# Encoder layer on one core: merged one-hot instructions, a bfloat16 position compare, 48 instead of 60 spilled u tiles, and two more raw buffers

## The chip, the core and the metric

The kernel runs on one core of a Trainium2 chip, and the metric is device time of one execution in microseconds (us). The core has five engines, each with its own instruction queue that runs strictly in order: PE (TensorE, matrix products; PEld is its loading of weights), DVE (VectorE), ACT (ScalarE), POOL (GpSimd) and SP (SyncE, which here only issues DMAs). Semaphores make an instruction wait for another engine or for a DMA. Of several runs the median counts.

## The reference, cut to what matters

One layer for 512 tokens and 16 meta tokens, model width 1024: a projection, two groups of attention-like heads, an output projection, and then PEER, a product-key lookup over 128 x 128 experts, which takes most of the time:

```
q = (x @ w_q).reshape(n, 8, 2, 128)
s = einsum('nhpc,hpkc->nhpk', q, sub_keys)
ts, ti = top_k(s, 16)                                  # per head, two halves
cand = ts[:,:,0,:,None] + ts[:,:,1,None,:]             # 16 x 16 sums
best_s, best_p = top_k(cand, 16)
idx  = (row index) * 128 + (column index)              # 16 experts per head
gate = softmax(best_s)
act  = gelu(einsum('nd,nhkd->nhk', x, u[idx]))
y    = einsum('nhk,nhkd->nd', gate * act, v[idx])
```

## The kernel before, in words

The first 128 tokens ("sparse quarter") are done as written: for each of 128 expert slots a row of u (later of v) per token is gathered by an indirect DMA that POOL issues (line 251, tile `gat`), and DVE multiplies and sums it (line 265 for u, line 263 for v). The other 384 tokens ("dense") are done for all 16,384 experts. u and v are cut into 128 tiles of 128 experts. A u tile gives 24 matmuls (lines 127 to 129) and a gelu on ACT (line 1055); a v tile gives 18 (lines 1080 to 1084). What weighs the experts is W, a dense matrix with the gates of the chosen experts and zeros elsewhere.

Precision: each fp32 operand is split in a high part (`hi`, cast on ACT, line 114) and a rest (`lo`, line 116), so each product is three matmuls. For the u tiles below `LA` the `lo` subtraction runs on POOL, for the others on DVE. A raw u tile comes by a DMA on SP's queue (line 108, `raw`, two buffers, given back when `lo` is done).

W is built 8 tokens at a time, 48 steps ("W steps", in `wbuild`). DVE compares row and column index of each choice with 0..127 (line 993, `oh<-iT,ioh`, two instructions of 128x1024 in fp16: one-hots), multiplies the first one-hot by the low and the high part of the gate (lines 994 and 996; in every fourth step the high part is done by ACT, line 999). PE multiplies the one-hots (lines 1021, 1022), ACT evacuates (line 1024, into `stg`), and after four steps a DMA on SP's queue stores `stg` to W_d in HBM (line 1026). The one-hots have four buffers.

Where the indices come from: `topk2` is called four times. In each, the position of a choice is compared with 0..15 (line 231, `eq`, 128x2048, fp32 inputs, twice per call) to pick the index.

Order of the second half of the program: the query products with their top-16 searches, then the *u phase* (u tiles 0 to LA-1 with their results spilled to A_d in HBM, and the W steps spread between them), then *v alone* (v tiles 0 to LA-1, which load W and A back), and then *u and v* (each v tile from LA on together with its u tile, nothing spilled). Before, LA is 60. No v tile can run before W is complete, six u tiles (`ET`) are kept for the end of that wait. The sparse quarter's 256 gathers are metered: RA per u tile in the u phase, RV per v tile while i < LA, RUV afterwards.

The row 0..127 that the one-hots are compared with is `iof` (64 KB, loaded on SP's queue, line 949). It lives in a pool, `wk`, whose memory is that of the query stage's score tiles, so its load waits until the last top-16 search has read them.

The order within an engine's queue is made by a scheduler at build time, from the order in which the program is written; the engines then keep it.

Of the kernel before, what the change touches and what calls it, by code (L numbers as in the profile page):

```python
# [9 lines left out]
F32 = mybir.dt.float32  # L10
# [14 lines left out]
P = 128  # L25
# [9 lines left out]
PH = 8  # L35
# [13 lines left out]
WL = 1  # L49
SC = 16  # L50
TK = 1, 1, 1, 1
# [10 lines left out]
VG = 6  # L62
RA = 0.4
RV = 0.85
RUV = 2.85
LA = 60
NCAND = 80
# [15 lines left out]
def _emit(ctx, tc, I, out):  # L83
# [105 lines left out]
    def topk2(a, b, sm, cand, tf, eq, zs):  # L189
# [35 lines left out]
        nc.vector.tensor_add(cf, cf, t1)  # L225
        nc.vector.tensor_sub(cf, cf, t9)
        nc.vector.tensor_scalar(rf, rf, -1.0, 0.0, op0=ALU.add, op1=ALU.max)
        nc.vector.tensor_add(rf, rf, t9)
        yield
        for j, pos in enumerate((rf, cf)):  # L230
            nc.vector.tensor_tensor(eq, pos[:, :, :, None].to_broadcast([P, PH, TOPK, TOPK]),
                                    io16[:, None, None, :].to_broadcast([P, PH, TOPK, TOPK]), op=ALU.is_equal)
            nc.vector.tensor_mul(eq, eq, tf[:, :, j, None, :].to_broadcast([P, PH, TOPK, TOPK]))
            nc.vector.tensor_add(eq[:, :, :, :8], eq[:, :, :, :8], eq[:, :, :, 8:])
            nc.vector.tensor_add(eq[:, :, :, :4], eq[:, :, :, :4], eq[:, :, :, 4:8])
            nc.vector.tensor_add(eq[:, :, :, :2], eq[:, :, :, :2], eq[:, :, :, 2:4])
# [710 lines left out]
    ioh = wk.tile([P, NK, QI], F16, name="ioh")  # L947
    iof = wk.tile([P, NK], F32, name="iof")
    nc.sync.dma_start(out=iof, in_=I["iota"].to_broadcast([P, NK]))
    nc.vector.tensor_copy(ioh, iof[:, :, None].to_broadcast([P, NK, QI]))  # L950
# [10 lines left out]
    def wbuild():  # L961
# [8 lines left out]
        def prep(t, m0):  # L970
            if m0 == 0:
                tr = bank((P, 3, P), tag="p")
                for j in range(3):
                    nc.tensor.transpose(out=tr[:, j, :], in_=sel[:, j, t].rearrange("p h r -> p (h r)"), identity=ident)
                gT = wk2.tile([P, P], F32, name="gT")
                nc.scalar.activation(gT, tr[:, 0, :], AF.Copy, scale=GS)
                iT = wk2.tile([P, 2, P], F16, name="iT")
                nc.scalar.copy(iT, tr[:, 1:3, :])
                gh = wk2.tile([P, P], F16, name="gh")
                nc.vector.tensor_copy(gh, gT)  # L980
                gl = wk2.tile([P, P], F16, name="gl")
                nc.vector.tensor_sub(gl, gT, gh)
                cur[t] = gT, iT, gh, gl
            gT, iT, gh, gl = cur[t]
            sh = [P, OB // QI, NK, QI]

            def tok(v):
                return v[:, m0:m0 + OB].rearrange("p (g q) -> p g q", q=QI)[:, :, None, :].to_broadcast(sh)

            oh = big.tile([P, 4] + sh[1:], F16, name="oh", tag=("hi0", "hi1", "lo0", "lo1")[(t * P + m0) // OB % WB])  # L990
            o12, ol, od = oh[:, :2], oh[:, 2], oh[:, 3]
            for j in range(2):
                nc.vector.tensor_tensor(o12[:, j], tok(iT[:, j]), ioh[:, None, :, :].to_broadcast(sh), op=ALU.is_equal)  # L993
            nc.vector.tensor_mul(ol, o12[:, 0], tok(gl))  # L994
            if m0 // OB % DM < DN:
                nc.vector.tensor_mul(od, o12[:, 0], tok(gh))  # L996
            else:
# [7 lines left out]
        for n, (t, m0) in enumerate(steps):  # L1005
# [19 lines left out]
            if q0 + OB == BL:  # L1025
                nc.sync.dma_start(out=W_d[:, ((t - 1) * P + m0) // BL], in_=stg)
            yield 2.2

    U, V = {}, {}
    gelus = []  # L1030

    def u_split(i):
        if i < NK and i not in U:
            U[i] = stream(I["uT"][i], eng=nc.gpsimd if i < LA and i % PU != PU - 1 else None)

# [232 lines left out]
```

## Time and profile before

| | us |
|---|---|
| runs: median (lowest to highest of 3) | 1678.32 (1671.53 to 1680.73) |
| the profiled execution: its own time | 1682.47 |
| the profiled execution: span from first to last instruction | 1680.7 |
| PE busy / DVE busy / ACT busy / POOL busy, of the span | 1574.4 / 1291.4 / 739.6 / 677.1 |

A profiled execution gives each instruction's start and end, what ended the idle time in front of it, and the granted TensorE clock (mean 0.973 of full speed here). A busy PE is not a PE at its peak, since matmuls overlap; the pace of PE is read from how many matmuls fall in a stretch. An instruction that is held up by another engine after it has started counts as busy: its duration is longer than that of its equals.

### The profile page before, as it was taken

Reading aid. Unit: us, or ns where it says so; the run is one execution under the profiler, and the core shown is the slowest. Engines: PE = TensorE matmul, PEld = TensorE weight load, DVE = VectorE, ACT = ScalarE, POOL = GpSimd, SP = SyncE. Lnnn points to the kernel's source line nnn. Section 1 sums busy time; section 2 is a strip of 40 time slices with the busy share of each in tenths; the row PEclk is TensorE's granted clock in tenths of the full one; section 3 lists DMA queues with packets and bytes.
Section 4 is the critical chain, followed back from the end, with each engine's and each line's share of the span. In section 5 each row is a group of like instructions: output and inputs, shape, how many; then the busy total and the mean of one; then the engine's idle time right before and its main releaser. Section 6 shows DMA issues by size and latency. Waiting matters only on the chain.

```text
span 1680.7 us, 24243 instructions
## 1 busy us (share of the span) xinstructions
PE 1574.4 (94%) x8793; PEld 1392.4 (83%) x8793; DVE 1291.4 (77%) x2529; ACT 739.6 (44%) x1229; POOL 677.1 (40%) x465
## 2 busy tenths in 40 slices
PE   6999998989986789979989999999999999999998
PEld 6888886768876689878978888889999999988996
DVE  3888768647999998948247777778887888778777
ACT  5454555543324474867533333333333333333334
POOL 3443112076334467475411212154545444344442
PEclk9999999989997989999999999999999999999999
DMA  6112222232224557656999999899999998999885
GB/s 232 54 46 81 69 61 69 84 118 89 78 73 149 176 193 250 239 218 252 328 366 342 326 314 326 278 313 389 321 329 326 336 327 315 319 339 327 308 276 185
DMA packets 152360, 387.42 MB, mean 231 GB/s; under 512 B 12752, under 2 KB 71376, under 8 KB 150576
## 3 DMA queue, kind: packets, MB, share of 16 engines
q1 hardware_dynamic: 106160, 238.79, 41.2%
q0 software_dynamic: 36864, 134.23, 22.8%
q10 hardware_dynamic: 9216, 12.85, 2.1%
q8 instruction: 69, 1.13, 0.3%
q14 instruction: 51, 0.42, 0.1%
HBM read 342.56 MB, written 40.63 MB: 228 GB/s over the span
## 4 chain that ended last, share of the span: by engine, by line
PE 28%; issue 18%; DVE 12%; POOL 10%; DMA 6%; ACT 3%; SPq 1%; POOLq 0%; ACTq 0%; DVEq 0%
POOL gat L251 7%; PE banka L1080 4%; PE banka L1083 4%; PE banka L1084 4%; POOL lo L116 3%; PE bankp L1080 2%; PE bankp L1083 2%; PE bankp L1084 2%; PE bankg L129 2%; DMA gat<-v,idx 2%; PE bankg L127 2%; PE bankg L128 2%; DMA raw<-uT 2%; DVE oh L993 2%; DMA gat<-u,idx 1%
## 5 line engine op out<-in xcount | busy, mean ns | idle before, releaser
L116 POOL TENSOR_TENSOR lo<-raw,hi 128x1024 fp32r<-128x1024 f32 x81 | 238.4, 2947 | 228.8 <-ACT hi L114 220.4
L114 ACT CAST hi<-raw 128x1024 fp32r<-128x1024 f32 x177 | 185.8, 1051 | 289.6 <-PE bankg L128 159.1
L127 PE MATMUL bankg<-un_hi,hi 128*128 128x384 f32 x880 | 300.1, 341 | 12.2 <-ACT act L1055 12.2
L129 PE MATMUL bankg<-un_hi,lo 128*128 128x384 f32 x880 | 299.6, 341 | 5.3 <-POOL lo L116 5.2
L128 PE MATMUL bankg<-un_lo,hi 128*128 128x384 f32 x880 | 297.9, 338 | 0.0
L251 POOL DMA_INDIRECT gat<-u,idx x128 | 157.8, 1232 | 299.5 <-PE bankp L1084 252.1
L251 POOL DMA_INDIRECT gat<-v,idx x128 | 167.8, 1311 | 207.6 <-PE bankp L1084 180.4
L263 DVE SCALAR_TENSOR_TENSOR acc<-gat,sact,acc 128x1024 f32<-128x1024 f32 x128 | 164.2, 1283 | 72.2 <-DMA gat<-v,idx 61.6
L265 DVE CUSTOM_DVE_ANT_0 gat<-gat,hn 128x1024 f32<-128x1024 f32 x128 | 162.9, 1282 | 53.2 <-DMA gat<-u,idx 53.1
L127 PEld LDWEIGHTS bankg<-un_hi,hi 128*128 128x128 f32 x880 | 168.1, 191 | 16.1 <-ACT act L1055 12.5
L135 DVE TENSOR_TENSOR vhl<-vraw,vhl 128x1024 fp32r<-128x1024 f32 x128 | 157.1, 1228 | 30.9 <-ACT vhl L134 30.8
L129 PEld LDWEIGHTS bankg<-un_hi,lo 128*128 128x128 f32 x880 | 167.9, 191 | 8.1 <-POOL lo L116 6.8
L128 PEld LDWEIGHTS bankg<-un_lo,hi 128*128 128x128 f32 x880 | 167.7, 191 | 3.4
L134 ACT CAST vhl<-vraw 128x1024 fp32r<-128x1024 f32 x128 | 134.2, 1049 | 46.3 <-PE bankp L1084 33.4
L116 DVE TENSOR_TENSOR lo<-raw,hi 128x1024 fp32r<-128x1024 f32 x96 | 117.8, 1228 | 24.2 <-ACT hi L114 23.0
L1024 ACT ACTIVATE stg<-banka 128x512 f32<-128x512 f32 x96 | 96.2, 1140 | 1.7 <-PE banka L1022 0.9
L993 DVE TENSOR_TENSOR oh<-iT,ioh 128x1024 f16<-128x1024 f16 x96 | 80.8, 888 | 2.4 <-PE banka L1022 2.4
L1021 PE MATMUL banka<-oh 128*128 128x128 f16 x384 | 55.3, 233 | 22.1 <-DVE oh L996 12.7
L1055 ACT ACTIVATE act<-bankg 128x384 f32<-128x384 f32 x110 | 53.4, 486 | 23.2 <-PE bankg L129 12.1
L1021 PEld LDWEIGHTS <-oh 128*128 128x128 f16 x384 | 39.2, 104 | 20.8 <-DVE oh L996 15.0
L1022 PE MATMUL banka<-oh 128*128 128x128 f16 x384 | 54.3, 233 | 0.7 <-DVE oh L994 0.7
L129 PE MATMUL bankp<-un_hi,lo 128*128 128x384 f32 x144 | 48.7, 338 | 4.5 <-POOL lo L116 4.5
(2283 smaller groups left out, 3906.3 us busy)
## 6 DMA issues: line engine op xcount, KB each, us to landing
raw<-uT SPq DMA_DIRECT2D x128, 512.0 KB
vraw<-v SPq DMA_DIRECT2D x128, 512.0 KB
W_d<-stg SPq DMA_DIRECT2D x12, 2048.0 KB
wa<-W_d SPq DMA_DIRECT2D x32, 768.0 KB
A_d<-act ACTq DMA_DIRECT2D x60, 192.0 KB
wa<-A_d SPq DMA_DIRECT2D x15, 768.0 KB
raw<-wq SPq DMA_DIRECT2D x16, 512.0 KB
raw<-win_n SPq DMA_DIRECT2D x12, 512.0 KB
```

The lines of the kernel that those rows point to most:

```text
L114: nc.scalar.copy(hi, raw)
L116: (eng or nc.vector).tensor_sub(lo, raw, hi.bitcast(F32))
L127: nc.tensor.matmul(o, lhsT=ah, rhs=bh, start=start, stop=False)
L128: nc.tensor.matmul(o, lhsT=ah, rhs=bl, start=False, stop=False)
L129: return nc.tensor.matmul(o, lhsT=al, rhs=bh, start=False, stop=stop)
L134: last[0] = nc.scalar.copy(hi, src).ins.name
L135: (eng or nc.vector).tensor_sub(lo, src, hi.bitcast(F32))
L251: g = nc.gpsimd.indirect_dma_start(out=r, out_offset=None, in_=src, in_offset=bass.IndirectOffsetOnAxis(ap=idx[:, hk:hk + 1], axis=0))
L263: nc.vector.scalar_tensor_tensor(acc0, r, sact[:, hk:hk + 1], acc0, op0=ALU.mult, op1=ALU.add)
L265: nc.vector.tensor_tensor_reduce(r, r, hn0, scale=1.0, scalar=0.0, op0=ALU.mult, op1=ALU.add, accum_out=sact[:, hk:hk + 1])
L993: nc.vector.tensor_tensor(o12[:, j], tok(iT[:, j]), ioh[:, None, :, :].to_broadcast(sh), op=ALU.is_equal)
L1080: m0 = nc.tensor.matmul(o, lhsT=gh_[:, tc_], rhs=vh[:, dc], start=(j == 0), stop=False, skip_group_check=True)
```

## The change

Seven edits:

1. `topk2`: the positions and the row 0..15 (`io16b`) are bfloat16, so both inputs and the output of the `eq` compare are 16 bit.
2. W steps: the two compares become one instruction of 128x2048; the two multiplies become one of 128x2048, except in every fourth step, where ACT still does the high part and DVE the low one (128x1024). The gates' two parts lie in one tile, `gs`.
3. LA 60 to 48. The metering of gathers goes from RA 0.4, RUV 2.85 to RA 0.15, RUV 2.7.
4. W_d stores are issued on ACT's queue.
5. `iof` moves to the pool `w1`, which lasts to the end of the program, and is loaded just ahead of the keys; the score tiles `sc` go from 16 to 15 buffers.
6. Odd u tiles from 9 to 41 are loaded into `rawx`, two more buffers in the pool `wk`.
7. A raw u tile is asked for four tiles ahead in the u phase (two before).

```diff
-SC = 16
+SC = 15
-RA = 0.4
+RA = 0.15
-RUV = 2.85
-LA = 60
+RUV = 2.7
+LA = 48
...
-        nc.vector.tensor_sub(cf, cf, t9)
+        nc.vector.tensor_sub(cb, cf, t9)
...
-        nc.vector.tensor_add(rf, rf, t9)
+        nc.vector.tensor_add(rb, rf, t9)
-        for j, pos in enumerate((rf, cf)):
+        for j, pos in enumerate((rb, cb)):
             nc.vector.tensor_tensor(eq, pos[:, :, :, None].to_broadcast([P, PH, TOPK, TOPK]),
-                                    io16[:, None, None, :].to_broadcast([P, PH, TOPK, TOPK]), op=ALU.is_equal)
+                                    io16b[:, None, None, :].to_broadcast([P, PH, TOPK, TOPK]), op=ALU.is_equal)
...
+    nc.vector.tensor_copy(io16b, io16)
...
+    iof = w1.tile([P, NK], F32, name="iof")
+    nc.sync.dma_start(out=iof, in_=I["iota"].to_broadcast([P, NK]))
     keys = qs.tile([P, 2 * PH, NK], F32, name="keys")
...
-    iof = wk.tile([P, NK], F32, name="iof")
-    nc.sync.dma_start(out=iof, in_=I["iota"].to_broadcast([P, NK]))
...
-            for j in range(2):
-                nc.vector.tensor_tensor(o12[:, j], tok(iT[:, j]), ioh[:, None, :, :].to_broadcast(sh), op=ALU.is_equal)
-            nc.vector.tensor_mul(ol, o12[:, 0], tok(gl))
-            if m0 // OB % DM < DN:
-                nc.vector.tensor_mul(od, o12[:, 0], tok(gh))
+            nc.vector.tensor_tensor(o12, tok(iT[:, blk].rearrange("p j m -> p (j m)")),
+                                    ioh[:, None, :, :].to_broadcast([P, 2 * GQ, NK, QI]), op=ALU.is_equal)
...
+            if blk % DM < DN:
+                nc.vector.tensor_mul(oh[:, 2 * GQ:].rearrange("p (c g) k q -> p c (g k q)", c=2).rearrange("p c (g k q) -> p c g k q", k=NK, q=QI),
+                                     o12[:, None, 0].to_broadcast([P, 2] + sh[1:]),
+                                     gs[:, blk].rearrange("p c (g q) -> p c g q", q=QI)[:, :, :, None, :].to_broadcast([P, 2] + sh[1:]))
             else:
+                nc.vector.tensor_mul(ol, o12[:, 0], tok(gs[:, blk, 1]))
...
-                nc.sync.dma_start(out=W_d[:, ((t - 1) * P + m0) // BL], in_=stg)
+                nc.scalar.dma_start(out=W_d[:, ((t - 1) * P + m0) // BL], in_=stg)
...
+    def u_fetch(i):
+        if i < NK and i not in U and i not in R:
+            if i % 2 and 8 <= i < LA - ET:
+                R[i] = wk.tile([P, 1024], F32, name="rawx", bufs=2)
+                nc.sync.dma_start(out=R[i], in_=I["uT"][i])
+            else:
+                R[i] = fetch(I["uT"][i])
...
         u_split(i + 2)
+        if i + 4 < LA:
+            u_fetch(i + 3)
+            u_fetch(i + 4)
```

The scheduler's order of the queues shows the edits at two places.

SP's queue before, where the u phase begins: loads of raw u tiles, and among them the load of the index row `iof`, which waits for DVE and PE (the names in brackets are the semaphores waited for).

```order
L108 DMA raw<-uT 128x1024 [waits DMAHW3_49,Pool_49]
L108 DMA raw<-uT 128x1024 [waits DMAHW4_49,Pool_49]
L949 DMA iof<-iota 128x128 [waits DVE_49,PE_49]
L108 DMA raw<-uT 128x1024 [waits DMAHW6_49,Pool_49]
L108 DMA raw<-uT 128x1024 [waits DMAHW5_49,DMAHW0_49,Pool_49]
```

The same place now, again after seven raw u tiles:

```order
L108 DMA raw<-uT 128x1024 [waits DMAHW4_49,Pool_49]
L108 DMA raw<-uT 128x1024 [waits DMAHW5_49,Pool_49]
L1047 DMA rawx<-uT 128x1024 [waits DVE_49,PE_49]
L1047 DMA rawx<-uT 128x1024
L108 DMA raw<-uT 128x1024 [waits DMAHW7_49,Pool_49]
L108 DMA raw<-uT 128x1024 [waits DMAHW1_49,Pool_49]
```

`iof` is gone from here, and in its row stands the first load into `rawx`, with a wait for the same two engines, since `rawx` lies in the same pool.

DVE's queue before, at the second of the three token tiles of W (`gh`, `gl` are the gates' parts, `oh` the one-hots, `gat` the gathered rows):

```order
L265 ISA gat,sact<-gat,hn_70 128x1024
L265 ISA sact 128x1
L980 CAST gh<-gT 128x128
L993 TENSOR_TENSOR oh<-iT,ioh 128x1024
L982 TENSOR_TENSOR gl<-gT,gh 128x128
L993 TENSOR_TENSOR oh<-iT,ioh 128x1024 x7
L996 TENSOR_TENSOR oh<-oh,gh 128x1024
L994 TENSOR_TENSOR oh<-oh,gl 128x1024
L265 ISA gat,sact<-gat,hn_70 128x1024
L265 ISA sact 128x1
```

The same place now:

```order
L985 CAST gs<-gT 128x16x8
L999 TENSOR_TENSOR oh<-iT,ioh 128x2048
L986 TENSOR_TENSOR gs<-gT,gs 128x16x8
L999 TENSOR_TENSOR oh<-iT,ioh 128x2048 x3
L1004 TENSOR_TENSOR oh<-oh,gs 128x2048 x3
L1008 TENSOR_TENSOR oh<-oh,gs 128x1024
L999 TENSOR_TENSOR oh<-iT,ioh 128x2048
L268 ISA gat,sact<-gat,hn_70 128x1024
L268 ISA sact 128x1
L999 TENSOR_TENSOR oh<-iT,ioh 128x2048
```

Four compares stand where eight stood, and gathers are used more rarely: three between the first and the last one-hot instruction of the program, fifteen before. In PE's queue 574 matmuls of u tiles stand between the first and the last matmul of the W steps, 895 before; ahead of the first stand 410, 377 before.

## Rows read from the trace of the kernel before

**Rows 1.** The page: busy time of each engine; PE and DVE in 40 slices
```profile
PE 1574.4 (94%) x8793; PEld 1392.4 (83%) x8793; DVE 1291.4 (77%) x2529; ACT 739.6 (44%) x1229; POOL 677.1 (40%) x465
...
PE   6999998989986789979989999999999999999998
...
DVE  3888768647999998948247777778887888778777
...
PEclk9999999989997989999999999999999999999999
```

**Rows 2.** Busy time by stretch: stretch, length, busy us (instructions), clock, DMA share, GB/s
```profile
474.00:558.00 84.00, 57.70 (x300) 55.73 (x299) 81.64 (x390) 27.09 (x37) 32.63 (x14) 0.82 0.33 107
558.00:804.00 246.00, 215.54 (x1644) 206.12 (x1644) 210.09 (x242) 163.58 (x259) 150.57 (x53) 0.95 0.64 230
816.00:836.00 20.00, 20.00 (x118) 20.00 (x117) 3.28 (x2) 7.62 (x10) 8.51 (x4) 1.00 1.03 362
846.00:1110.00 264.00, 263.82 (x1174) 220.32 (x1175) 193.09 (x279) 96.67 (x134) 50.41 (x50) 0.99 0.93 320
1125.00:1440.00 315.00, 315.00 (x1595) 286.90 (x1594) 259.91 (x327) 112.35 (x154) 151.57 (x111) 1.00 0.94 335
```

**Rows 3.** DVE's groups, 558 to 804: busy us, mean ns | idle before, its end
```profile
L993 DVE TENSOR_TENSOR oh<-iT,ioh 128x1024 f16<-128x1024 f16 x96 | 80.8, 888 | 2.4 <-PE banka L1022 2.4
L994 DVE TENSOR_TENSOR oh<-oh,gl 128x1024 f16<-128x1024 f16 x48 | 43.4, 908 | 0.0
L996 DVE TENSOR_TENSOR oh<-oh,gh 128x1024 f16<-128x1024 f16 x36 | 33.2, 924 | 0.0
L265 DVE CUSTOM_DVE_ANT_0 gat<-gat,hn 128x1024 f32<-128x1024 f32 x15 | 26.2, 1745 | 30.6 <-DMA gat<-u,idx 30.6
L233 DVE TENSOR_TENSOR eq<-eq,tf 128x2048 bf16<-128x2048 bf16 x4 | 7.0, 1739 | 0.1
L234 DVE TENSOR_TENSOR eq<-eq 128x1024 bf16<-128x1024 bf16 x4 | 6.9, 1727 | 0.1
L231 DVE TENSOR_TENSOR eq<-sm_cf,io 128x2048 bf16<-128x2048 f32 x2 | 4.6, 2286 | 0.0
L231 DVE TENSOR_TENSOR eq<-sm_rf,io 128x2048 bf16<-128x2048 f32 x2 | 4.6, 2277 | 0.0
```

**Rows 4.** Single lines' durations, ns: shortest/median/longest, first and last start
```profile
L993 DVE TENSOR_TENSOR oh<-iT,ioh x96: 672/679/3277, 558.8 to 802.7; 128x1024 f16<-128x1024 f16 x96
...
L265 DVE CUSTOM_DVE_ANT_0 gat<-gat,hn x16: 1207/1226/3424, 567.2 to 809.1; 128x1024 f32<-128x1024 f32 x16
...
L116 POOL TENSOR_TENSOR lo<-raw,hi x56: 2342/2434/12507, 473.1 to 830.2; 128x1024 fp32r<-128x1024 f32 x56
...
L233 DVE TENSOR_TENSOR eq<-eq,tf x8: 1211/1270/3301, 462.4 to 642.9; 128x2048 bf16<-128x2048 bf16 x8
```

**Rows 5.** DVE in order of time, 587 to 589: start us, us, instruction
```profile
587.28 1.28 DVE L993 TENSOR_TENSOR oh<-iT,ioh 128x1024 f16<-128x1024 f16 x2
588.48 0.68 DVE L994 TENSOR_TENSOR oh<-oh,gl 128x1024 f16<-128x1024 f16 x1
```

**Rows 6.** POOL's groups, 558 to 804
```profile
L116 POOL TENSOR_TENSOR lo<-raw,hi 128x1024 fp32r<-128x1024 f32 x38 | 133.3, 3513 | 85.8 <-ACT hi L114 77.5 <-PE banka L1022 8.2
```

**Rows 7.** SP's queue, 474 to 804: who waited for whom: us, times, longest
```profile
SPq L1026 <- ACT stg L1024: 24.6, 9, 8.2
SPq L949 <- DVE tiv L187: 21.3, 1, 21.3
```

**Rows 8.** The engines' waits, 558 to 804
```profile
ACT hi L114 <- DMA raw<-uT: 32.4, 11, 5.5
```

**Rows 9.** ACT's queue in order of time, 475: an issue of an A_d store
```profile
474.84 0.35 ACTq L1057 DMA_DIRECT2D A_d<-act  x1
```

**Rows 10.** DVE in order of time at the start, with the idle time before
```profile
21.01 0.79 DVE L330 SCALAR_TENSOR_TENSOR act_lo<-xT,ln,act_hi 128x528 fp32r<-128x528 f32 x1 [7.40 <-ACT act_hi L329]
```

**Rows 11.** Busy time by stretch: PE during two W steps
```profile
600.42:602.24 1.82, 1.82 (x33) 1.81 (x33) 1.82 (x2) 1.80 (x3) 1.82 (x2) 1.00 0.08 7
```

**Rows 12.** The chain of waits within 558 to 804, by line
```profile
by line: POOL lo L116 17.8%; issue 17.1%; DMA raw<-uT 12.0%; DVE oh L993 11.2%; DMA gat<-u,idx 6.3%; ACT stg L1024 3.6%; PE bankg L129 3.2%; PE bankg L127 3.0%; ACT oh L999 2.9%; PE banka L1021 2.8%; PE bankg L128 2.8%; ACT hi L114 2.8%; PE
```

More of the change, by code (lines that the diff above doesn't have):

```diff
@@ L155, in _emit @@
     io16 = cst.tile([P, TOPK], F32, name="io16")
+    io16b = cst.tile([P, TOPK], BF, name="io16b")
     def half(name, tag, j, n):
@@ L218, in topk2 @@
         cf = sm("cf")
+        rb = sm("rb", BF)
+        cb = sm("cb", BF)
         nc.vector.tensor_copy(rf, row)
@@ L976, in prep @@
                 nc.scalar.activation(gT, tr[:, 0, :], AF.Copy, scale=GS)
[L977 to L985, printed above, removed]
@@ L987, in tok @@
-            def tok(v):
-                return v[:, m0:m0 + OB].rearrange("p (g q) -> p g q", q=QI)[:, :, None, :].to_broadcast(sh)
-            oh = big.tile([P, 4] + sh[1:], F16, name="oh", tag=("hi0", "hi1", "lo0", "lo1")[(t * P + m0) // OB % WB])
-            o12, ol, od = oh[:, :2], oh[:, 2], oh[:, 3]
-            for j in range(2):
-                nc.vector.tensor_tensor(o12[:, j], tok(iT[:, j]), ioh[:, None, :, :].to_broadcast(sh), op=ALU.is_equal)
-            nc.vector.tensor_mul(ol, o12[:, 0], tok(gl))
@@ L995, in prep @@
-            if m0 // OB % DM < DN:
-                nc.vector.tensor_mul(od, o12[:, 0], tok(gh))
+                iT = wk2.tile([P, P // OB, 2, OB], F16, name="iT")
+                nc.scalar.copy(iT.rearrange("p b j m -> p j b m"), tr[:, 1:3, :].rearrange("p j (b m) -> p j b m", m=OB))
+                gs = wk2.tile([P, P // OB, 2, OB], F16, name="gs")
+                g8 = gT.rearrange("p (b m) -> p b m", m=OB)
+                nc.vector.tensor_copy(gs[:, :, 0, :], g8)
+                nc.vector.tensor_sub(gs[:, :, 1, :], g8, gs[:, :, 0, :])
@@ new lines, in prep @@
+                cur[t] = gT, iT, gs
+            gT, iT, gs = cur[t]
+            GQ = OB // QI
+            sh = [P, GQ, NK, QI]
+            def tok(v):
+                n = v.shape[1] // QI
+                return v.rearrange("p (g q) -> p g q", q=QI)[:, :, None, :].to_broadcast([P, n, NK, QI])
+            oh = big.tile([P, 4 * GQ, NK, QI], F16, name="oh", tag=("hi0", "hi1", "lo0", "lo1")[(t * P + m0) // OB % WB])
+            o12 = oh[:, :2 * GQ]
+            blk = m0 // OB
+            nc.vector.tensor_tensor(o12, tok(iT[:, blk].rearrange("p j m -> p (j m)")),
+                                    ioh[:, None, :, :].to_broadcast([P, 2 * GQ, NK, QI]), op=ALU.is_equal)
@@ new lines, in prep @@
+            o12 = o12.rearrange("p (j g) k q -> p j g k q", j=2)
+            od, ol = oh[:, 2 * GQ:3 * GQ], oh[:, 3 * GQ:]
+            if blk % DM < DN:
+                nc.vector.tensor_mul(oh[:, 2 * GQ:].rearrange("p (c g) k q -> p c (g k q)", c=2).rearrange("p c (g k q) -> p c g k q", k=NK, q=QI),
+                                     o12[:, None, 0].to_broadcast([P, 2] + sh[1:]),
+                                     gs[:, blk].rearrange("p c (g q) -> p c g q", q=QI)[:, :, :, None, :].to_broadcast([P, 2] + sh[1:]))
@@ L1025, in wbuild @@
             if q0 + OB == BL:
-                nc.sync.dma_start(out=W_d[:, ((t - 1) * P + m0) // BL], in_=stg)
+                nc.scalar.dma_start(out=W_d[:, ((t - 1) * P + m0) // BL], in_=stg)
             yield 2.2
-    U, V = {}, {}
+    U, V, R = {}, {}, {}
     gelus = []
+    def u_fetch(i):
[5 more added lines that the diff above has]
+                R[i] = fetch(I["uT"][i])
     def u_split(i):
         if i < NK and i not in U:
-            U[i] = stream(I["uT"][i], eng=nc.gpsimd if i < LA and i % PU != PU - 1 else None)
+            u_fetch(i)
+            U[i] = stream(I["uT"][i], raw=R.pop(i), eng=nc.gpsimd if i < LA and i % PU != PU - 1 else None)
     def v_split(i):
```

## The prediction

> **What bounds the kernel now.** I read the page first, then the busy time by stretch, then the waits and the single lines inside the one stretch that is not bound by PE.
>
> The page has PE busy 94% of the span, and its slices show where it isn't: around the middle third, where DVE's slices are full [rows 1]. The stretches say it sharper [rows 2]. From 846 on (v alone) PE is busy 263.8 of 264 us, and from 1125 on (u and v) 315.0 of 315. There one v tile with one u tile is 42 matmuls, and 1595 matmuls in 315 us make 8.29 us a pair. The u phase alone shows 118 matmuls in 20.00 us, so 24 of them take 4.07. I take 4.15, half a pair, for a u tile, wherever it stands. So behind the u phase the time is PE's work alone, and each u tile that is moved there costs 4.15 us in full.
>
> In the W stretch, 558 to 804 (first to last one-hot instruction, 246 us), DVE is busy 210.1 us, and what it lacks is nearly all one wait: 30.6 us for gathered rows [rows 2, 3]. DVE is in order, so a gather that comes late stops the one-hots behind it, and they stop PE's W matmuls. But its busy time is not all its own. A one-hot takes 679 ns at the median and 3277 at the longest, 2.6 us more, about one `lo` on POOL (median 2434, longest 12507) [rows 4]. The two engines hold each other up. Counted over the means, DVE's stretching is (888-679)x96 + (908-679)x48 + (924-679)x36 + (1745-1226)x15 + (1739-1211)x4 + (1727-679)x4 ns = 54 us, spread over 38 `lo` of POOL, 1.42 us each [rows 3, 4, 6]. So the W stretch is DVE's own work, plus what POOL takes from it, plus the waits for gathers.
>
> **The change part by part.** The sum is made against the profiled execution, 1682.5 us, of which the span is 1680.7. It lies 4.2 us above the median of the runs, 1678.3.
>
> *The bfloat16 compare.* A compare of 128x2048 with fp32 inputs takes 2.28 us, the multiply of the same size with 16-bit operands 1.21 at the shortest [rows 3, 4]. That is 1.07 us each, four times before the W stretch and four times in it: 4 us each. DVE has 81.6 of 84 us busy before the stretch [rows 2], so both count.
>
> *One-hots.* 48 pairs of compares and 36 pairs of multiplies become 84 instructions of twice the size. By durations a pair gives back 2x0.679 - 1.21 = 0.15 us, 12 us in all. By starts it is less: two follow each other within 1.20 us though each lasts 0.68 [rows 5], and if the large one overlaps its successor by the same 0.08, it takes 1.13. That is 0.07 us a pair, 6 us. I take 6, since the pace counts and not the duration. The bounds are 0 and 12.
>
> *Fewer gathers in the W stretch.* DVE's order holds 3 there for 15. Twelve fewer at 1.23 us are 15 us of work. Their waits, 12/15 of 30.6 us, are 24 us. The gathers move to the last stage, where DVE has 260 of 315 us busy and PE is the bound [rows 2], and cost nothing there: RUV 2.7 over 80 tiles keeps less per tile than 2.85 over 68.
>
> *Thirteen u tiles fewer in the W stretch.* PE's order holds 574 u matmuls between first and last W matmul for 895, 13.4 tiles. So POOL has some 25 `lo` there for 38. At 1.42 us each that gives DVE back 18 us. But POOL did part of its work while DVE stood waiting for gathers, and with those waits gone that work falls on DVE too. I take 12 us, bounds 0 and 32 (13 times the whole 2.43).
>
> The Trainium skill's page "SBUF — State Buffer", section "SBUF: two separate sides", says that VectorE with two SBUF inputs and GpSimd share one port pair under an exclusive lock that is held for a whole instruction. The longest one-hot, its own 0.68 and a whole `lo`, agrees; by that rule in full the term is 32 and not 12, which is the first rival below.
>
> *The price: 12 u tiles behind the u phase.* 12 x 4.15 = +50 us, all on PE, which has no idle time there. Their spills to A_d and back fall away, and they lie beside PE's work in both places, 0.
>
> *Stores on ACT's queue.* SP stood 24.6 us in nine waits for the last part of `stg`, with raw loads behind it [rows 7]. ACT now issues the twelve stores behind its own evacuation, at about 0.35 us each [rows 9], 4 us beside 163.6 of 246 us busy [rows 2]; nothing on its queue waits longer than that. SP's gain is a raw load that comes earlier. ACT waited 32.4 us for raw tiles in the stretch [rows 8], and those loads are 12% of its chain [rows 12], but DVE lost no time other than to gathers and POOL, so I count 0. The cover is DVE's work: if it shrinks further than I think, PE's tiles show next.
>
> *Two more buffers, four tiles ahead.* For the same reason 0. And one wait changes its name only: SP stood 21.3 us at the load of `iof`, until the last top-16 search gave its score tile free [rows 7]. Now the first `rawx` load stands in that very place with the same wait, and all raw loads stand behind it as before. I count nothing for moving `iof`.
>
> *Small things.* The new copy `io16b` waits for its DMA in DVE's queue ahead of the last parts of the input, where DVE is idle 7.40 us [rows 10]: 0. Fifteen score buffers: the sixteenth copy waits for the first tile's readers, first in DVE's order: 0.
>
> *Sum.* Before the stretch -4. In it -6 -4 -15 -24 -12 = -61, so that 246 becomes 185. Behind it +50. Together -15: 1667.5 for such an execution, and less the 4.2, 1663 for the median.
>
> **The rivals.**
>
> *A: each `lo` takes its whole 2.43 us from DVE, or the raw loads were on the path.* POOL's 13 `lo` are worth 32 us, the stretch becomes 165, and the time 1643. For it: the longest one-hot, and POOL and raw loads as two of the three largest parts of the chain [rows 4, 12]. Against it: DVE's stretching measured 1.42 us a `lo`, not 2.43 [rows 3, 6].
>
> *B: PE becomes the floor of the W stretch.* Two W steps take PE 1.82 us [rows 11], 48 take 44. Before, 37.3 u tiles at 4.15 make 155, together 199 of 246 us, so 47 were lost to waiting in order. Now 23.9 tiles make 99, with W 143; if the same 47 are lost, and the first W matmul comes 6 us later since 410 u matmuls stand ahead of it and not 377, the stretch takes 196. That is -50 in place of -61: 1674, no change. For it: u and W matmuls share one in-order queue. Against it: most of the lost time was DVE's lateness, which is what shrinks.
>
> *C: slower. DVE waits in another place.* With longer instructions DVE keeps POOL out longer, `lo` comes late, PE's tile stands in front of the W matmuls, and the four one-hot buffers come free late. Then gathers' waits turn into waits for PE, and POOL's share gives nothing: only 6 + 4 + 15 = 25 us are left in the stretch. -4 -25 +50 = +21: 1699. It decides from the point where the stretch shrinks by less than 46 us, to over 200. Against it: DVE waited for PE only 2.4 us in 96 one-hots [rows 3]. For it: a `lo` was already held up to 12.5 us [rows 4].
>
> *D: the change does not do what it says.* The merged forms and the new compare take 2.28 us, like the fp32 compare of that size. 84 x 2.28 + 12 x 0.68 = 200 us for 122, and nothing from the compare: some +85 on 1663, 1748. Against it: the present one-hot has the same inner pair of elements and takes 0.68 us for half the size [rows 4, 5].
>
> **How the numbers follow.** My forecast (1650 to 1676) gets 0.50, A 0.18, B 0.18, C 0.10, D 0.04. The forecast is 1663. The measurement of this kernel can tell about 0.5% from no change, 8.4 us: faster is under 1670, slower over 1687. Faster: 0.8 of the forecast, A, and a little of B, 0.61. Slower: most of C, D and a little of B, 0.13. The same: 0.26. The range for 8 in 10 runs from A's middle, a little below it, to between B and C: 1638 to 1690. The terms' own bounds (0 to 12, 0 to 32) lie inside.
>
> **What the changed profile would show.** The W stretch, first to last one-hot instruction, at 185 us, under 200 in any case for a gain; merged one-hots at about 1.2 us at the median, the compare also; DVE's wait for gathers there under 8 us; still one raw load with a wait of some 20 us on DVE near 480; the stages behind at 8.29 us a pair and PE without idle time. A median of 2.2 us at the one-hots would be D; waits of DVE for PE in the tens of us C. If the stretch takes 165 or less, my term for POOL was too small. If u and v together take more than 8.4 us a pair, the price is wrong.

## The result: slower by 0.9%, and the profile after

The changed kernel takes 1691.81 us (median of 5 runs, 1691.65 to 1695.35), beside 1678.32 for the kernel before (1671.53 to 1680.73). The ratio over all runs is 1.0093, 95% interval 1.0069 to 1.0118 (the medians alone give 1.0080). I had forecast 1663, with a range up to 1690: the sign was wrong, and the time lies outside the range.

The profiled execution after takes 1691.9 us, its span is 1690.1. The page of the changed kernel, the same lines as [rows 1]:

```profile
PE 1584.6 (94%) x8793; PEld 1397.7 (83%) x8793; DVE 1281.3 (76%) x2458; ACT 737.7 (44%) x1229; POOL 637.9 (38%) x453
...
PE   7999999989976868997999999999999999999998
...
DVE  3888767647999978891577778877777787777786
...
PEclk9999997989998888999999999999999999999999
```

The middle part in which PE isn't full is shorter, and the full part behind it longer. I cut both executions at the same four events, each read from its instructions in order of time: the end of the first u tile's gelu, the first one-hot, the last one-hot, the first v matmul.

| part of the span, us | before | after | change | forecast |
|---|---|---|---|---|
| up to the first gelu | 474.8 | 479.1 | +4.3 | 0 |
| first gelu to first one-hot | 84.0 | 94.8 | +10.8 | -4 |
| first to last one-hot | 245.2 | 186.9 | -58.3 | -61 |
| last one-hot to first v matmul | 42.2 | 40.1 | -2.1 | 0 |
| first v matmul to the end | 834.5 | 889.2 | +54.7 | +50 |
| span | 1680.7 | 1690.1 | +9.4 | -15 |

The W stretch came within 3 us of the forecast, and the kernel is slower all the same. The second row shows why this proves less than it seems: the stretch begins where DVE gets to its first one-hot, and DVE gets there later. The busy time by stretch after (stretch, length, then busy us of PE, PEld, DVE, ACT and POOL, clock, DMA share, GB/s), to be read beside [rows 2]:

```profile
479.00:574.00 95.00, 66.49 (x345) 64.67 (x344) 95.00 (x392) 29.26 (x40) 40.10 (x15) 0.84 0.34 116
574.00:761.00 187.00, 161.13 (x1343) 152.48 (x1342) 161.63 (x129) 146.18 (x233) 91.75 (x28) 0.94 0.59 217
801.00:1010.00 209.00, 209.00 (x926) 174.51 (x927) 152.19 (x221) 76.29 (x105) 38.07 (x38) 0.99 0.92 320
1040.00:1440.00 400.00, 398.01 (x2004) 360.10 (x2003) 312.99 (x403) 140.40 (x195) 168.37 (x130) 1.00 0.90 319
```

DVE is busy 95.00 of 95 us ahead of the one-hots. With 392 instructions there as against 390 before, it takes 13 us more for as many. DVE's groups between the first and the last one-hot, beside [rows 3] (busy us, mean ns | idle before, its end):

```profile
L999 DVE TENSOR_TENSOR oh<-iT,ioh 128x2048 f16<-128x2048 f16 x48 | 67.9, 1442 | 0.0
L1004 DVE TENSOR_TENSOR oh<-oh,gs 128x2048 f16<-128x2048 f16 x36 | 64.5, 1818 | 0.1
L1008 DVE TENSOR_TENSOR oh<-oh,gs 128x1024 f16<-128x1024 f16 x12 | 12.6, 1047 | 0.1
L268 DVE CUSTOM_DVE_ANT_0 gat<-gat,hn 128x1024 f32<-128x1024 f32 x4 | 4.9, 1216 | 12.1 <-DMA gat<-u,idx 12.1
```

Single lines' durations after (ns: shortest/median/longest, first and last start), beside [rows 4]:

```profile
L999 DVE TENSOR_TENSOR oh<-iT,ioh x48: 1203/1211/3457, 574.0 to 758.9; 128x2048 f16<-128x2048 f16 x48
...
L1004 DVE TENSOR_TENSOR oh<-oh,gs x36: 1209/1212/3466, 580.8 to 755.5; 128x2048 f16<-128x2048 f16 x36
...
L234 DVE TENSOR_TENSOR eq<-sm_rb,io16b x4: 2268/2276/4384, 462.9 to 585.2; 128x2048 bf16<-128x2048 bf16 x4
L234 DVE TENSOR_TENSOR eq<-sm_cb,io16b x4: 2271/3280/4489, 481.8 to 621.8; 128x2048 bf16<-128x2048 bf16 x4
...
L116 POOL TENSOR_TENSOR lo<-raw,hi x52: 2349/2402/12819, 34.2 to 811.1; 128x1024 fp32r<-128x1024 f32 x52
```

The merged one-hots take 1.21 us, as forecast. The bfloat16 compare takes 2.28 where nothing holds it up, as the fp32 one did: all its operands have 16 bits now, and it gained nothing. The longest compare and one-hots still lie 2.2 us over those times, nearly a `lo` of POOL.

Two more views, the waits of DVE between the first gelu and the last one-hot, and of SP's queue there (us, times, longest), beside [rows 3, 7]:

```profile
DVE gs L985 <- ACT gT L980: 12.8, 2, 7.2
DVE gat L268 <- DMA gat<-u,idx: 12.1, 1, 12.1
```

```profile
SPq L108 <- POOL lo L116: 127.8, 20, 20.7
SPq L1047 <- POOL lo L116: 109.1, 15, 19.4
SPq L1047 <- DVE tiv L188: 21.3, 1, 21.3
```

The gathers' wait is 12.1 us, not under 8, and another has grown beside it: DVE waits 12.8 us for ACT to copy the transposed gates, 2.5 before. The first raw load into the new buffers (L1047) has inherited the 21.3 us, as forecast. And SP's other loads wait for POOL, which has not used the buffers yet: asking earlier doesn't help where the reader is late.

The +4.3 at the front is there by 304 us already (a load of `wo` that SP issues at 303.8 before and at 308.0 after), and PE's clock goes with it. Ten microseconds well before the u phase, first of the kernel before, then after:

```profile
280.00:290.00 10.00, 10.00 (x39) 6.59 (x38) 6.11 (x15) 6.36 (x20) 0.00 (x0) 0.83 0.05 11
```

```profile
280.00:290.00 10.00, 10.00 (x28) 6.53 (x28) 4.14 (x10) 4.22 (x13) 0.00 (x0) 0.50 0.00 1
```

The granted clock is 0.50 here after, the lower of its two levels (1.2 GHz), and a full-busy PE does 28 matmuls for 39. By their starts, the same matmuls stand 1.4 us earlier after than before near 270 us, and 4.3 us later from some 300 on.

### The profile page after: what moved, and what is told of

Read it like the earlier page. It is cut to its first block, busy times and chain, and to the rows that moved or that the text cites. A ratio compares the mean times of both kernels' runs of the same rounds, so it can differ in the third digit from the quotient of the medians.

```text
span 1690.1 us, 24084 instructions
## 1 busy us (share of the span) xinstructions
PE 1584.6 (94%) x8793; PEld 1397.7 (83%) x8793; DVE 1281.3 (76%) x2458; ACT 737.7 (44%) x1229; POOL 637.9 (38%) x453
## 4 chain that ended last, share of the span: by engine, by line
issue 24%; PE 15%; POOL 9%; DVE 8%; DMA 6%; ACT 2%; SPq 1%; POOLq 0%; ACTq 0%; DVEq 0%
POOL gat L254 9%; DMA gat<-v,idx 3%; DVE oh L999 3%; PE banka L1104 2%; PE banka L1100 2%; PE banka L1103 2%; DMA gat<-u,idx 2%; DVE oh L1004 2%; PE bankg L129 1%; PE bankg L128 1%; PE bankg L127 1%; PE bankp L1103 1%; PE bankp L1100 1%; PE bankp L1104 1%; DVE gat L268 1%
## 5 line engine op out<-in xcount | busy, mean ns | idle before, releaser
L127 PE MATMUL bankg<-un_hi,hi 128*128 128x384 f32 x912 | 310.2, 340 | 17.1 <-ACT act L1075 17.1
L129 PE MATMUL bankg<-un_hi,lo 128*128 128x384 f32 x912 | 310.2, 340 | 6.6 <-POOL lo L116 6.6
L128 PE MATMUL bankg<-un_lo,hi 128*128 128x384 f32 x912 | 309.4, 339 | 0.0
L114 ACT CAST hi<-raw 128x1024 fp32r<-128x1024 f32 x160 | 168.0, 1051 | 214.8 <-PE bankg L128 136.2
L116 POOL TENSOR_TENSOR lo<-raw,hi 128x1024 fp32r<-128x1024 f32 x52 | 151.3, 2911 | 174.0 <-ACT hi L114 160.2
L116 DVE TENSOR_TENSOR lo<-raw,hi 128x1024 fp32r<-128x1024 f32 x108 | 132.4, 1226 | 17.0 <-ACT hi L114 16.2
L116 POOL TENSOR_TENSOR lo<-rawx,hi 128x1024 fp32r<-128x1024 f32 x17 | 49.1, 2887 | 73.2 <-ACT hi L114 73.1
L1032 PE MATMUL banka<-oh 128*128 128x128 f16 x384 | 53.2, 227 | 19.9 <-DVE oh L1004 15.0
L999 DVE TENSOR_TENSOR oh<-iT,ioh 128x2048 f16<-128x2048 f16 x48 | 67.9, 1442 | 0.0
L1004 DVE TENSOR_TENSOR oh<-oh,gs 128x2048 f16<-128x2048 f16 x36 | 64.5, 1818 | 0.1
```

Of the source, the lines that this page charges most:

```text
L114: nc.scalar.copy(hi, raw)
L116: (eng or nc.vector).tensor_sub(lo, raw, hi.bitcast(F32))
L127: nc.tensor.matmul(o, lhsT=ah, rhs=bh, start=start, stop=False)
L128: nc.tensor.matmul(o, lhsT=ah, rhs=bl, start=False, stop=False)
L129: return nc.tensor.matmul(o, lhsT=al, rhs=bh, start=False, stop=stop)
L999: nc.vector.tensor_tensor(o12, tok(iT[:, blk].rearrange("p j m -> p (j m)")), ioh[:, None, :, :].to_broadcast([P, 2 * GQ, NK, QI]), op=ALU ...
```

## The experiments

Theory S: the trade of the tiles lost. The 12 u tiles cost 52 to 55 us behind and gave back less in the W stretch, since DVE is the bound there, and neither the gathers' waits nor the compare gave what I took from them. Rival P: the early raw loads spoil the W stretch, since ACT's casts for them stand ahead of the gelus. (After, PE waited 17.1 us in one piece for a gelu, until 513.9; before 12.2.) Parts are given as in the table above, from the profiled executions; "middle" is from the first gelu to the first v matmul. Ratios are to runs of the kernel before made beside each experiment, whose medians are 1678.9 to 1680.1.

| kernel | to first gelu | middle | from v on | span | median of runs |
|---|---|---|---|---|---|
| before | 474.8 | 371.4 | 834.5 | 1680.7 | 1678.3 |
| e2: before, three numbers changed | 475.8 | 336.3 | 886.8 | 1698.9 | 1704.0 |
| e11: before, one-hots merged | 478.8 | 356.8 | 832.8 | 1668.5 | 1671.2 |
| after | 479.1 | 321.8 | 889.2 | 1690.1 | 1691.8 |
| e1: after, the three numbers of before | 471.6 | 360.5 | 833.9 | 1666.0 | 1671.6 |
| e3: after, no early loads | 477.7 | 326.5 | 886.0 | 1690.2 | 1692.8 |
| e4: after, fp32 compare | 477.4 | 322.2 | 891.3 | 1690.8 | 1692.6 |
| e5: after, no `lo` on POOL | 473.9 | 264.0 | 893.4 | 1631.3 | 1624.8 |
| e6: after, 8 gathers back | 477.9 | 326.4 | 892.9 | 1697.3 | 1694.6 |
| e7: e1 with 10 gathers fewer | 479.5 | 348.6 | 830.5 | 1658.6 | 1659.4 |
| e8: e7 with LA 68 | 477.5 | 378.9 | 821.4 | 1677.8 | 1677.8 |
| e9: e7, `lo` on DVE | 483.9 | 326.1 | 830.5 | 1640.5 | 1645.1 |
| e10: e7, every second `lo` on DVE | 484.4 | 328.0 | 830.6 | 1643.0 | 1647.4 |
| e12: e9, positions in pairs | 485.1 | 320.0 | 831.4 | 1636.5 | 1638.8 |

**The trade alone, and everything but the trade (e2, e1).** The edits are the same three lines, once put into before, once taken out of after:

```
-RA = 0.4     +RA = 0.15
-RUV = 2.85   +RUV = 2.7
-LA = 60      +LA = 48
```

> The changed kernel with the three numbers of before (LA 60, RA 0.4, RUV 2.85), so that merged one-hots, bfloat16 compare, raw loads and the stores on ACT stay and the 12 u tiles go back into the W stretch. Theory S (the trade of the tiles loses): the 12 tiles cost 54.7 us behind the u phase and give back only some 47 us, counted from the first u tile's gelu to the last one-hot; without the trade the merges and the rest of the edits are left, some 6 to 15 us: 1663 to 1675, at least 0.5% faster than before. Rival P (the early raw loads spoil the W stretch: their casts stand ahead of the gelus on ACT, PE's u tiles are late): it stays at 1685 or over, since the loads are still there.

> The kernel before with LA 48, RA 0.15 and RUV 2.7 alone. Theory S: +55 behind the u phase, and 36 us of gathers and their waits leave the W stretch: 1690 to 1705, at or above the changed kernel. Rival P: without the early loads the W stretch shrinks by the whole 61 us that was forecast: 1675 or under.

e1 is 0.9952 of before (0.9933 to 0.9971), e2 1.0154 (1.0128 to 1.0180). Theory S holds, P falls: without the trade the changed kernel is 8 us faster than before, and the trade alone is 25 us slower. In the table it costs 52.3 and 55.3 us from v on and gives back 35.1 and 38.7 in the middle.

**Early loads and compare (e3, e4).** Undone one at a time in the changed kernel:

```
 def u_fetch(i):
...
-            if i % 2 and 8 <= i < LA - ET:
-                R[i] = wk.tile([P, 1024], F32, name="rawx", bufs=2)
...
-        if i + 4 < LA:
-            u_fetch(i + 3)
-            u_fetch(i + 4)
```

> The changed kernel without the early loads: no rawx buffers, nothing asked for four tiles ahead. Theory S: the loads were not on the path, 1688 to 1696. Rival P: PE no longer waits 17 us for the gelu of u tile 4 behind the casts on ACT, and the first one-hot comes 10 us earlier: 1675 to 1683.

```
-        for j, pos in enumerate((rb, cb)):
+        for j, pos in enumerate((rf, cf)):
...
-                                    io16b[:, None, None, :]
+                                    io16[:, None, None, :]
```

> The changed kernel with the fp32 compare of before in place of the bfloat16 one (positions and index row in fp32, io16b gone). The trace of the changed kernel has the compare at 2.28 us as before, so theory S expects no change: 1688 to 1696. If the bfloat16 compare is worth its forecast 1.07 us times eight all the same (the changed trace being disturbed by POOL), it becomes 1700.

1692.8 and 1692.6 beside 1691.8: neither moves the time. In e3 the first one-hot does come earlier (89.3 us behind the first gelu, not 94.8), and the stretch behind it is 9.8 us longer: the place of the border moved, not the work. P falls here too. DVE's waits change their names once more in e3: 0.3 us for gathers in place of 12.1, and 21.5 us for PE to give one-hot buffers back, of which the changed kernel shows none.

**Gathers (e6, e7).** From here on S has a sharper form, theory T: DVE is the bound of the middle, and each `lo` on POOL holds it up. Its rival G: the gathers set the middle, and `lo` fits into DVE's gaps. The number of u tiles stays in each pair; only RA and RUV move gathers between the W stretch and the last stage:

```
 e6, on after:            e7, on e1:
-RA = 0.15   +RA = 0.4    -RA = 0.4    +RA = 0.15
-RUV = 2.7   +RUV = 2.6   -RUV = 2.85  +RUV = 3.05
```

> The changed kernel with RA 0.4 and RUV 2.6: some 8 gathers come back into the W stretch from the last stage, the number of u tiles stays. My prediction priced a gather there at 1.23 us of DVE's work and 2 us of wait (39 us for twelve): then 8 of them add 26 us, 1715 to 1722. Theory T: their waits are filled by POOL's lo, which then cost DVE nothing, so a gather adds about its own work and a part of the wait, 1 to 2 us each: 1698 to 1708.

> The changed kernel with LA 60, RA 0.15 and RUV 3.05: no u tile is moved, some 10 gathers go from the W stretch to the last stage; beside LA 60 with RA 0.4 (1671.6). By my prediction's price of a gather (3.25 us) 34 us go from the stretch: 1638. Theory T: 10 to 20 us go, 1651 to 1662. If the last stage has no room for 0.2 more gathers a pair (its DMA busy over 0.9), the gain is given back there: 1668 or over.

Eight gathers back cost 2.7 us by the medians, 4.6 in the middle and nothing by the ratios (1.0081, after 1.0093, each within 0.3%), not 26, and less than the 6 that T has at the least: at LA 48 a gather costs less than its own work. Ten away give 12.2 us by the medians and 11.9 in the middle, 1.2 each: a gather's own work [rows 4] and nothing of its wait. What became of the waits is in the window from the first gelu to the last one-hot, e1 first, then e7:

```profile
472.00:790.00 318.00, 269.21 (x1928) 259.52 (x1927) 298.84 (x538) 190.92 (x293) 171.95 (x66) 0.92 0.60 209
```

```profile
479.00:786.00 307.00, 264.79 (x1925) 256.18 (x1924) 286.06 (x526) 191.05 (x295) 168.60 (x56) 0.92 0.57 198
```

DVE's busy time falls by 12.8 us, its idle time stays (19.2 and 20.9). Its waits there, again e1 and then e7, changed their names: that for gathers fell, that for ACT's `gT` rose.

```profile
DVE gat L268 <- DMA gat<-u,idx: 12.6, 3, 10.3
...
DVE gs L985 <- ACT gT L980: 2.1, 1, 2.1
```

```profile
DVE gs L985 <- ACT gT L980: 9.3, 2, 8.5
DVE gat L268 <- DMA gat<-u,idx: 7.7, 1, 7.7
```

e7 also says that the last stage has room for these gathers: 830.5 us from v on, and it is faster than before at no price, 0.9877 (0.9852 to 0.9903).

**POOL's lo (e5).** A cost taken away whole:

```
         hi = stm.tile([P, 1024], F32R, name="hi", tag="hi", bufs=bufs)
         nc.scalar.copy(hi, raw)
+        if eng is not None:
+            return hi, hi
```

> The changed kernel without POOL's lo of the first 48 u tiles: hi stands in for lo in their matmuls, so the low parts of these u tiles are left out of the result, with as many matmuls as before. Theory T (DVE is the bound and every lo holds it up; fewer tiles there free it by what they held): the trace of the changed kernel has DVE some 80 us over its medians beside 77 lo between the first u tile's gelu and the last one-hot, so this part goes from 282 us to 215 to 240 us, where PE's own u and W matmuls (some 230) are next: 1635 to 1655. Rival G (gathers alone set it, POOL's lo fit into DVE's gaps): 270 us or more, 1680 or over.

The edit reaches further than that: POOL makes `lo` for 48 u tiles and for 21 weight tiles ahead of them, 16 of them of `w_q`, and in e5 for none of the 69, so all their low parts are left out. And the trace of the changed kernel has 39 `lo` of POOL between the first gelu and the last one-hot, not 77. 1624.8, 67 us less than after, more than T expected; by the profiled executions it is 58.8, of which 57.8 in the middle. The part from the first gelu to the last one-hot takes 222.6 us, which is T's 215 to 240, and G falls with its 270. From 340, ahead of the whole top-16 search, to the last one-hot, after and then e5:

```profile
340.00:761.00 421.00, 358.55 (x2326) 327.28 (x2326) 360.14 (x1028) 229.47 (x357) 211.99 (x93) 0.92 0.43 154
```

```profile
340.00:696.00 356.00, 334.43 (x2259) 306.54 (x2258) 280.24 (x1024) 221.99 (x347) 44.47 (x35) 0.98 0.52 180
```

DVE has 1028 and 1024 instructions there and is busy 79.9 us less: 58 `lo` of POOL, 42 of u tiles and 16 of `w_q`, which are no work of DVE's, make its own work longer by 1.4 us each. The last 44 of them count for more. They stand where DVE is busy 290.6 of 316 us, and there it is 71.3 us, 1.6 each; again after, then e5:

```profile
445.00:761.00 316.00, 261.56 (x1866) 246.91 (x1866) 290.63 (x667) 189.15 (x292) 145.44 (x48) 0.91 0.48 172
```

```profile
439.00:696.00 257.00, 243.20 (x1826) 230.88 (x1825) 219.31 (x662) 183.74 (x286) 13.14 (x4) 0.99 0.60 211
```

PE's granted clock rises from 0.91 to 0.99 along with it, and what part of the gain that makes was not separated. The step from e7 to after goes the same way by tiles: the middle goes from 348.6 to 321.8, which is 26.8 us for 12, 2.2 each, with the tiles' matmuls and two gathers in it.

**More tiles, not fewer (e8).**

```
-LA = 60     +LA = 68
-RUV = 3.05  +RUV = 3.3
```

> The changed kernel with LA 68, RA 0.15 and RUV 3.3: eight more u tiles in the W stretch than at LA 60, none of the price. Beside the run with LA 60 and RA 0.15 it wins 8 times 4.4 to 4.6 us behind, 36 us, and pays what 8 tiles cost in the W stretch. Theory T: a tile costs there 1.5 to 2.5 us (a lo on POOL beside a busy DVE, PE's matmuls partly in gaps), so it is 16 to 24 us faster than that run. If a tile costs as much there as behind, no change; if the last stage has no room for the gathers, slower.

18 us slower than e7. The middle grows by 30.3, 3.8 us a tile and not 1.5 to 2.5: T's price of a tile does not carry over to tiles beyond 60. From the first v matmul to the last gelu e8 takes 32.6 us less than e7 (781.8 and 814.4), as eight tiles should, but behind the last gelu 39.6 us for 16.0. That end, from 1638 on:

```profile
L266 DVE SCALAR_TENSOR_TENSOR acc<-gat,sact,acc 128x1024 f32<-128x1024 f32 x15 | 19.3, 1284 | 4.4 <-DMA gat<-v,idx 4.0
L254 POOL DMA_INDIRECT gat<-v,idx x11 | 12.8, 1166 | 4.1 <-issue 2.4 <-DVE acc L266 0.7 <-DMA gat<-v,idx 0.7
```

These are gathers that the last stage did not get done beside its tiles. So at LA 68 the stage has no room for 0.25 more of them a pair than in e7.

**lo on DVE (e9, e10).** In e7:

```
-eng=nc.gpsimd if i < LA and i % PU != PU - 1 else None
+eng=None                     (e10 instead: PU = 2 for 100)
```

> The run with LA 60 and RA 0.15 (1659.4 us), with every lo of the u phase on DVE and none on POOL. Theory T (a lo on POOL holds DVE up for 2.2 us, nearly its whole length): DVE does it itself in 1.22 us, as it does in the last stage, so 49 of them give back some 48 us; some of it is lost where lo now stands in DVE's order behind pieces of the top-16 search and PE waits for it: 1615 to 1645. Rival G (POOL's work was hidden but for 1.1 us a lo): no change or slower, 1655 to 1675.

> The same with every second lo of the u phase on DVE. Theory T: about half of what the whole gives, 1635 to 1655. Rival G: 1655 to 1668.

1645.1, 0.9794 of before (0.9776 to 0.9812): 14 us less than e7, at the very end of T's 1615 to 1645; G, with 1655 or more, falls here too. DVE's `lo` in e9, first gelu to last one-hot; the busy time of e9 from 340, and from its first gelu, to the last one-hot, and of e7 from 340; and the one-hots of e9:

```profile
L116 DVE TENSOR_TENSOR lo<-raw,hi 128x1024 fp32r<-128x1024 f32 x28 | 34.1, 1219 | 9.1 <-ACT hi L114 8.9 <-DMA rawx<-uT 0.2
L116 DVE TENSOR_TENSOR lo<-rawx,hi 128x1024 fp32r<-128x1024 f32 x22 | 27.0, 1228 | 7.2 <-ACT hi L114 7.2
```

```profile
340.00:766.00 426.00, 393.31 (x2524) 363.63 (x2523) 353.23 (x1081) 241.76 (x371) 102.55 (x53) 0.95 0.49 171
...
484.00:766.00 282.00, 261.29 (x1891) 251.87 (x1890) 245.18 (x532) 189.46 (x290) 31.23 (x6) 0.96 0.61 214
```

```profile
340.00:786.00 446.00, 395.72 (x2565) 366.31 (x2564) 389.70 (x1032) 245.29 (x379) 248.29 (x106) 0.93 0.48 166
```

```profile
L999 DVE TENSOR_TENSOR oh<-iT,ioh x48: 1205/1220/1252, 572.6 to 763.1; 128x2048 f16<-128x2048 f16 x48
...
L1004 DVE TENSOR_TENSOR oh<-oh,gs x36: 1205/1220/1251, 580.5 to 761.9; 128x2048 f16<-128x2048 f16 x36
```

With POOL out of the way no one-hot is stretched: the longest is 1.25 us and not 3.46. Some 53 `lo` have gone over to DVE there (POOL's instructions fall from 106 to 53), its count grows by 49, and it is busy 36.5 us less. An estimate from these rows: in e7 each of them cost DVE (36.5 + 53 x 1.22) / 53 = 1.9 us. The middle shrinks by 22.5, of which 4.4 come back ahead of the first gelu. PE is now busy 261 of 282 us from the first gelu to the last one-hot, which makes it the likely next bound; no run shows that. e10 has half of the `lo` on DVE and nearly the whole gain, 1647.4, which T had halfway; why half is almost enough stays open.

**The merge alone (e11).** The hunk on the one-hots of the change, put into before:

```
-            for j in range(2):
-                nc.vector.tensor_tensor(o12[:, j], tok(iT[:, j]), ...)
+            nc.vector.tensor_tensor(o12, tok(iT[:, blk].rearrange("p j m -> p (j m)")), ...)
```

> The kernel before with the merged one-hots alone. My prediction's term: 6 us less, bounds 0 and 12, so 1668 to 1675 with before at 1679.5. Rival R (what the changed kernel has left at LA 60, 8 us, comes from the raw loads, the earlier index row or the stores on ACT): 1677 to 1682.

1671.2, 0.9953 of before (0.9934 to 0.9973). It is within half a microsecond of e1, so raw loads, index row, stores on ACT and compare are together worth nothing at LA 60 that runs with an interval of 0.2% to either side can show, and the merge 8 us. The stretch from the first gelu to the last one-hot and the gathers' wait in it, to be read beside [rows 2, 3]:

```profile
478.00:793.00 315.00, 266.73 (x1933) 257.02 (x1932) 300.17 (x547) 190.97 (x293) 171.59 (x66) 0.93 0.59 208
```

```profile
DVE gat L265 <- DMA gat<-u,idx: 7.2, 2, 6.9
```

All 15 gathers are still there, and their wait is 7.2 us for 30.6. But DVE is busy 300.2 us, not 291.7, though the merge took work from it. So that wait was no fixed price of a gather, and most of it did not come back as time: DVE stands still less, and is held up longer beside the same 50 `lo`.

**A compare that is faster (e12).** In e9, the positions are written twice side by side, and the compare runs over pairs:

```
-        nc.vector.tensor_sub(cb, cf, t9)
+        nc.vector.tensor_sub(cb.rearrange("p h (a q) -> p h a q", q=2), two(cf), two(t9))
...
-            nc.vector.tensor_tensor(eq, pos[:, :, :, None].to_broadcast([P, PH, TOPK, TOPK]),
+            nc.vector.tensor_tensor(eq.rearrange("p h a (b q) -> p (h a) b q", q=2),
+                  pos.rearrange("p h (a q) -> p (h a) q", q=2)[:, :, None, :].to_broadcast([P, PH * TOPK, TOPK // 2, 2]), ...
```

> The run with LA 60, RA 0.15 and every lo on DVE (1645.1 us), with the positions of the bfloat16 compare written twice side by side, so that no operand of the compare repeats one element along its innermost axis, as in the one-hots. Theory I (it was this repeated element that kept the bfloat16 compare at 2.28 us): the compare takes 1.21 us, eight of them give back 8 us of DVE's work, of which the four or five ahead of the first one-hot count in full and the rest is partly beside PE: 1637 to 1643. Rival K (a compare that writes bfloat16 is as slow in any layout): 2.28 us and no change, or a little slower by the two longer writes.

```profile
L237 DVE TENSOR_TENSOR eq<-sm_row,io16b x4: 1203/1218/1234, 460.8 to 592.1; 128x2048 bf16<-128x2048 bf16 x4
L237 DVE TENSOR_TENSOR eq<-sm_bp,io16b x4: 1194/1218/1234, 475.9 to 629.1; 128x2048 bf16<-128x2048 bf16 x4
```

1.22 us for 2.28, with the same types and sizes: theory I holds. The time is 1638.8 us, 0.9755 of before (0.9728 to 0.9782), the shortest of all but e5, which leaves work out, 41 us under the runs of before beside it and 53 under the changed kernel.

## Why the prediction was wrong

**The steps that failed.** The trade was to cost +50 and bring, with gathers and POOL's share, -51, so nothing. It cost 52 to 55 and brought 35 to 39.

*"Fewer gathers in the W stretch": -39, measured -12 (e7) for ten, and in the middle -5 for eight at LA 48 (e6).* Of the 15 us of work 12 were there in e7. The 24 us of waits were not: I treated DVE's idle time at one wait as time that comes back, and another wait took its place (e7), or POOL held DVE up longer (e11).

*"Thirteen u tiles fewer": -12, measured -27 (e1 with e7's gathers, to after).* This erred the other way, near my bound of 32. With the tiles moved first it is more: from e1 to e6, which moves 12 tiles and 4 gathers, the middle loses 34.1 us. So how the 39 us divide depends on the order, and in either order the gathers had too much of it and the tiles too little. The mean stretch of 1.42 us a `lo` came from an execution in which DVE also stood idle for 38 us [rows 2] and part of POOL's work fell there. With DVE more nearly always busy it is 1.6 a `lo` (e5) or 1.9 (e7, by e9), and 2.2 a tile in all (e7 to after). The Trainium skill's page "SBUF — State Buffer", section "SBUF: two separate sides", has the lock held for a whole instruction; the stretched one-hots agree (3.46 for 1.21 us, beside a `lo` of 2.40), and so does e9, where they are gone. In the mean a `lo` cost 1.6 to 1.9 us of its 2.40.

*"The bfloat16 compare": -8, measured 0 (e4).* I priced it by a multiply of the same size and types, whose operands repeat over an outer axis; the compare's positions repeat along the innermost one. e12 shows that this was the whole cause. The Trainium skill's page "VectorE: DVE Perf Modes", section "What auto-detection actually checks", asks for 16-bit tensors with a step of one element, and an operand that repeats has none: 2.28 and 1.22 us agree with it. My rival D had named the compare at 2.28, but tied it to the one-hots, where it did not happen.

*"The price": +50, measured +54.7, and +52.3 in e2.* I had taken half a pair from the best stretch. The rows of before had more: from the 65th to the 128th gelu it needs 531.1 us, 8.43 a pair, and a v tile alone takes 4.05 (18 of 1174 matmuls in 264 us [rows 2]), so a u tile moved there costs 4.38, and twelve 52.6. Its pairs are a little slower besides: the median is 8.31 us in both, but the changed kernel needs 534.7 us for the same stretch. What makes single pairs late is not settled.

*The front: 0, measured +4.3.* e1 and e7 issue the same instructions in the same order up to the u phase, and reach the first gelu at 471.6 and 479.5. The 4.3 us are less than what equal streams differ by, so they can't be put down to the change. Another 4.1 us of the error lie in the base: the profiled execution before was that much above its median, the one after only 0.1.

By parts the error of 28.8 us is 15.4 in the middle (-49.6 for -65), 4.7 behind, 4.3 at the front and 4.1 in the base, 28.5 in all.

**What held.** Merged one-hots at 1.21 us, and the merge worth 8 us of 6 (0 to 12) forecast (e11). Nothing to be seen from raw loads, index row, io16b, and stores on ACT (e3, e11). The inherited wait of 21.3 us. PE without idle time behind. Rival C had the sign and nearly the time (1699) but not the mechanism: DVE's wait for PE was no part of it, and where it is (e3) the time is the same. Rival D's sum leaves out the 8 us of the compare that it speaks of: 92 and not 85. The rule "under 200 us for a gain" was a bad test, since the stretch it measured begins at an event that DVE's own lateness moves; from the first gelu on the gain was 49.6 us, under the price.

## What to carry to other kernels

Cut a span at events that the change can't move, or sum over the neighbours too. An in-order engine's idle time at one wait is not a gain in hand. Work that goes away is a better measure, and even that counted whole in one place (e7) and less than half in another (e6). Before work is moved out of a bound stage to a stage that another engine fills, ask what it costs in each and whether the bound engine can be freed where it stands: here it paid to give POOL's work back to DVE, which takes half as long there, and the trade didn't pay at all.

## What the runs showed of the hardware

An element-wise subtraction of 128x1024 in fp32 takes 1.22 us on DVE and 2.40 on POOL, and on POOL it also lengthens DVE's instructions beside it by up to 2.25 us (3.46 for 1.21): with 53 of them moved to DVE, DVE was busy for less time. That is not only so of two inputs. A cast of 128x128 took 1.21 us in the mean after, and 0.24 in e5 with no `lo` on POOL; the top-16 search's MAX8 was not lengthened (0.28 after, 0.29 to 0.30 in e5). A 128x2048 compare with three 16-bit operands takes 2.28 us if one operand repeats each element along the innermost axis, and 1.22 if that axis has pairs of neighbours. PE's clock was 1.00 in one execution and 0.50 in another, at a place that e1 and e7 reach by the same instructions in the same order; of e1 and then e7:

```profile
280.00:290.00 10.00, 9.72 (x38) 6.01 (x38) 8.27 (x23) 7.57 (x28) 0.00 (x0) 1.00 0.23 77
```

```profile
280.00:290.00 10.00, 9.58 (x27) 6.06 (x27) 4.18 (x10) 3.69 (x12) 0.12 (x1) 0.50 0.12 26
```

In the ten microseconds ahead of this PE was busy 6.0 of 10 us in e1 and 6.5 in e7. Across this place, from e1's 267 to its 292, e7 falls from 4.4 to 9.5 us behind e1, by the starts of the same matmuls. What decides between the two levels these runs don't show.
